# Experts of a two-layer model: the token blocks of an expert share each weight unit in turn, one code arm for each count class

## The chip, the cores and the metric

The kernel runs on one core of one Trainium2 chip. The metric is device microseconds of one execution, the median of several runs of the same program.

## The reference

Two layers of a hybrid model. Each mixes tokens (gated linear attention, differential attention, pooling) and then sends every token through two of sixteen experts. The first layer does so for 1280 tokens (256 context, 1024 latent), the second for the 1024 latent ones. Only the expert part matters here, cut to its core:

```python
def hier_moe(h, wg, bg, we, be, w1, w3, w2):        # h (N, 1024)
    g_prob = softmax(h @ wg + bg)                    # 4 groups, the best is taken
    e_prob = softmax(logits of the 4 experts in that group)   # the best 2 are taken
    weights = g_top * e_top / sum(e_top)
    ...                                              # assignments sorted by expert
    yb = (silu(x @ w1[e]) * (x @ w3[e])) @ w2[e]     # w1, w3 (1024, 512), w2 (512, 1024)
    out.at[token].add(yb * weight)                   # each token: sum over its experts
```

All of it is float32. How many rows an expert gets is known only at run time.

## The kernel before

A float32 product is made of three fast ones. `split` (L63, L64) writes a high part (ScalarE copy to the matmul's rounded type) and a low part (VectorE, value less high part); `mm3` (L67 to L69) adds high x high, high x low and low x high in PSUM.

For each layer the router leaves the list of rows of each expert and its count in memory. The stage then goes through the 16 experts in a fixed order. The weights of one expert are 12 units of 128 x 1024 numbers (512 KB): 0 to 3 and 4 to 7 hold w1 and w3 for the two halves of the hidden width, 8 to 11 hold w2. `fetch` has SyncE load a unit into one of 8 buffers `eraw`; `load_unit` has ScalarE copy its high part (L1579) and VectorE, for every third unit GpSimd, subtract the low part (L1581), into one of 13 buffers `ew`.

The rows of an expert are worked in blocks of 128. Block 0 (`x0`) always runs. The extra rows have their own blocks ahead of it: over 192 rows a full block 1; over 320 a full block 2, between 256 and 320 a 64-row block 2; between 128 and 192 a 64-row block 1. The prediction names the classes by their blocks: f (one full block), fh (a full and a 64-row one), ff, ffh, fff. Branches at run time (lines L1821, L1831, L1853, L1856 in the profile) choose, on each engine for itself. Rows beyond 384 go through a loop that this input never enters.

`gather` fetches a block's rows (GpSimd, indirect DMA) into `xg`. `prep` turns them: four TensorE transposes for each half (L1609) into a PSUM tile `xtp`, split by ScalarE and VectorE into `x`. A second VectorE instruction (L1611, CAST) copies 64 rows of the low part beside the high part, which only a 64-row block reads: it multiplies both parts in one pass (`pass2`). `prep` runs for blocks 0 and 1 of every expert, and for block 2 over 192 rows, whether the block is used or not.

`block` runs a full block through all 12 units. After units 0 to 3 ScalarE and VectorE make `g` = silu(h1) x h3 (L1653, L1654), TensorE turns `g` (L1636) in the middle of the next units, and the split is `ghl`. So there is a chain of TensorE, ScalarE, VectorE, TensorE, ScalarE, VectorE, TensorE for each half, the second of which ends at units 8 to 11. At the end VectorE weighs the result and GpSimd adds the rows to the output by an indirect DMA (L1626).

Only during block 0, the last of its expert, does `side(u)` load the 12 units of the next expert (one for each unit used), turn its blocks 0 and 1 at units 4, 5, 8 and 9, and issue gathers. `tc.manual_schedule()` keeps every engine's instructions in the order written:

```python
at = (6, 7, 9, 10) if ei == 0 else (4, 5, 8, 9)
if u in at:
    j, q = divmod(at.index(u), 2)
    if q == 0:
        nx["p"] = prep(gg[j], (x2, x1)[j])
    nx["p"](q, ("xtp", "hpse")[q])
```

Of the kernel before, what the change touches and what calls it, by code (L numbers as in the profile page):

```python
# [20 lines left out]
P = 128  # L21
# [34 lines left out]
def backbone_kernel(ctx: ExitStack, tc: tile.TileContext, x, ctx_in, cond, w_mod, b_mod, norm1, norm2, w_in_t, w_in_vg,  # L56
# [91 lines left out]
    for l in range(depth):  # L148
# [717 lines left out]
        ast, pst = ExitStack(), ExitStack()  # L866
        with ExitStack() as st:
# [685 lines left out]
        with ExitStack() as st:  # L1553
# [3 lines left out]
            RAW = 8  # L1557
            YT = 3
            early = True
            xg2 = mp1.tile([P, D], F32, name="xg2")  # L1560
# [4 lines left out]
            eo = [EPG * g + i for i in range(EPG) for g in (0, 2, 1, 3)]  # L1565
            seq = [(e, u) for e in eo for u in range(NUNIT)]
            raws = []

            def fetch():
                if seq:  # L1570
                    e, u = seq.pop(0)
                    raw = wk.tile([P, D], F32, name="eraw", tag="eraw", bufs=RAW)
                    nc.sync.dma_start(out=raw, in_=experts[l, e, u])
                    raws.append(raw)
# [12 lines left out]
            for _ in range(RAW):  # L1587
                fetch()
            def gather(idx, tag):
                g = wk.tile([P, D], F32, name="xg", tag=tag, bufs=YT if tag == "yt" else 1)  # L1590
                nc.gpsimd.indirect_dma_start(out=g, out_offset=None, in_=h2s,
                                             in_offset=bass.IndirectOffsetOnAxis(ap=idx, axis=0))
                return g

            gg = [None, None]
            for b in (1, 0):
                gg[b] = gather(ix[:, eo[0] + b * NE:eo[0] + b * NE + 1], f"xg{b}")
            units = [load_unit(u, False, nc.gpsimd if u in (3, 6) else nc.vector) for u in range(7)]
            for _ in range(7):
                fetch()  # L1600
            xt_ = [[mp1.tile([P, KD, n], F32R, name=f"x{n}{i}") for n in (P + P // 2, P)] for i in range(3)]

            def prep(g, xt):
# [17 lines left out]
            def scatter(yt, y, n, w, yidx):  # L1621
# [401 lines left out]
```

## Time and profile before

| | |
|---|---|
| median of 3 runs | 2952.78 us (2952.75 to 2956.32) |
| span of the profiled execution | 2951.4 us |
| TensorE busy | 2558.9 us, 87% |
| VectorE busy | 1911.1 us, 65% |
| ScalarE busy | 1243.7 us, 42% |
| GpSimd busy | 865.3 us, 29% |
| mean granted TensorE clock | 0.928 of full |
| expert stage, layer 0 | 936.5 to 1559.8 us of the span |
| expert stage, layer 1 | 2340.8 to 2920.5 us |

The profile is of one execution, so its span is compared with itself and the median stands beside it. The page's busy times are of all stages, and what bounds the experts is read in their two stretches: what each engine does there, what TensorE waits for, and what ends the wait. In rows with "<-" the name behind the arrow released the engine named ahead of it; "PEq" is TensorE's own sequencer, whose branches are listed as "PEldq COMPARE_BRANCH".

### The profile page before, as it was taken

Reading aid. Unit: us, or ns where it says so; the run is one execution under the profiler, and the core shown is the slowest. Engines: PE = TensorE matmul, PEld = TensorE weight load, DVE = VectorE, ACT = ScalarE, POOL = GpSimd, SP = SyncE. Lnnn points to the kernel's source line nnn. Section 1 sums busy time; section 2 is a strip of 40 time slices with the busy share of each in tenths; the row PEclk is TensorE's granted clock in tenths of the full one; section 3 lists DMA queues with packets and bytes.
Section 4 is the critical chain, followed back from the end, with each engine's and each line's share of the span. In section 5 each row is a group of like instructions: output and inputs, shape, how many; then the busy total and the mean of one; then the engine's idle time right before and its main releaser. Section 6 shows DMA issues by size and latency. Waiting matters only on the chain. (4 is left out here: it accounts for less than half of the span.)

```text
span 2951.4 us, 41503 instructions
## 1 busy us (share of the span) xinstructions
PE 2558.9 (87%) x15412; PEld 2145.6 (73%) x15412; DVE 1911.1 (65%) x3175; ACT 1243.7 (42%) x2060; POOL 865.3 (29%) x576
## 2 busy tenths in 40 slices
PE   6999998888896888789887999979989787978885
PEld 4878888887785667667666898868978566756664
DVE  3305765767578777876874317758867767687775
ACT  3322214665235444544554322137643354445453
POOL 0001113302244444443440001122024444454442
PEclk8999999999897999899998999989989888989997
DMA  8372227321336666776766252273122668587765
GB/s 286 131 259 104 76 77 191 69 65 51 116 128 230 217 212 201 243 239 183 233 191 214 84 178 76 80 178 77 42 94 104 229 192 288 174 301 235 236 216 196
DMA packets 159574, 494.08 MB, mean 167 GB/s; under 512 B 18896, under 2 KB 40016, under 8 KB 158768
## 3 DMA queue, kind: packets, MB, share of 16 engines
q1 hardware_dynamic: 110336, 361.14, 37.0%
q0 software_dynamic: 29312, 99.39, 12.1%
q10 hardware_dynamic: 19552, 28.84, 2.7%
q8 instruction: 201, 3.29, 0.5%
q14 instruction: 173, 1.42, 0.1%
HBM read 408.75 MB, written 79.15 MB: 165 GB/s over the span
## 5 line engine op out<-in xcount | busy, mean ns | idle before, releaser
L1581 DVE TENSOR_TENSOR ew<-eraw,ew 128x1024 fp32r<-128x1024 f32 x256 | 408.7, 1615 | 46.8 <-ACT ew L1579 39.9
L1579 ACT ACTIVATE ew<-eraw 128x1024 fp32r<-128x1024 f32 x384 | 390.4, 1053 | 107.1 <-PE hps L69 90.1
L1581 POOL TENSOR_TENSOR ew<-eraw,ew 128x1024 fp32r<-128x1024 f32 x128 | 331.4, 2598 | 126.9 <-issue 84.6
L67 PE MATMUL hps<-ew,x 128*128 128x512 f32 x656 | 280.0, 427 | 79.8 <-PEq L1856 75.7
L212 PE MATMUL ps<-hh,w 128*128 128x256 f32 x2096 | 287.2, 291 | 18.1 <-ACT hh L319 5.5
L212 PEld LDWEIGHTS ps<-hh,w 128*128 128x128 f32 x2096 | 267.4, 196 | 27.5 <-issue 7.9
L69 PE MATMUL hps<-ew,x 128*128 128x512 f32 x656 | 269.2, 410 | 10.7 <-DVE x L64 6.8
L68 PE MATMUL hps<-ew,x 128*128 128x512 f32 x656 | 269.1, 410 | 1.4 <-issue 1.4
L962 DVE TENSOR_REDUCE mx<-S 128x1 f32<-128x1280 f32 (+1 forms) x144 | 196.9, 1370 | 106.7 <-PE S L957 105.2
L1626 POOL DMA_INDIRECT xb<-yt,yx x54 | 131.7, 2440 | 412.5 <-DVE yt L1625 231.3
L67 PEld LDWEIGHTS hps<-ew,x 128*128 128x128 f32 x656 | 131.5, 200 | 114.4 <-issue 87.5
L970 ACT ACTIVATE pe<-S,mx 128x1280 f32<-128x1280 f32 (+1 forms) x144 | 177.5, 1232 | 48.2 <-DVE mx L962 40.9
L1611 DVE CAST x<-x 128x256 fp32r<-128x256 f32 x146 | 177.5, 1216 | 5.0
L956 PE MATMUL S<-kk,qh 128*128 128x512 f32 (+1 forms) x400 | 159.5, 399 | 16.0 <-DMA qh<-qs 7.8
L69 PE MATMUL yps<-ew,ghl 128*128 128x512 f32 x328 | 137.6, 420 | 40.6 <-DVE ghl L64 40.6
L69 PEld LDWEIGHTS hps<-ew,x 128*128 128x128 f32 x656 | 130.9, 200 | 45.2 <-DVE x L64 8.1
L68 PEld LDWEIGHTS hps<-ew,x 128*128 128x128 f32 x656 | 132.0, 201 | 26.7
L212 PE MATMUL ps<-hl,w 128*128 128x256 f32 x1048 | 149.7, 286 | 0.0
L67 PE MATMUL yps<-ew,ghl 128*128 128x512 f32 x328 | 143.3, 437 | 0.0
L67 PE MATMUL ps<-wv,hh 128*128 128x256 f32 (+1 forms) x480 | 142.2, 296 | 0.0
L957 PE MATMUL S<-kk,ql 128*128 128x512 f32 (+1 forms) x400 | 141.7, 368 | 0.3 <-DMA ql<-qs 0.3
L69 PE MATMUL ps<-wv,hl 128*128 128x256 f32 (+1 forms) x480 | 138.0, 288 | 0.0
(597 smaller groups left out, 5841.8 us busy)
## 6 DMA issues: line engine op xcount, KB each, us to landing
eraw<-in_experts_dram SPq DMA_DIRECT2D x384, 512.0 KB
s<-in_w_mod_dram SPq DMA_DIRECT2D x91, 512.0 KB
raw<-in_w_in_t_dram SPq DMA_DIRECT2D x28, 512.0 KB
xb<-xt POOLq DMA_DIRECT2D x18, 512.0 KB, 2.9
h2s<-tm POOLq DMA_DIRECT2D x18, 512.0 KB, 2.9
kk<-ks SPq DMA_DIRECT2D x14, 640.0 KB
ks<-shl ACTq DMA_DIRECT2D x16, 512.0 KB
qs<-shl ACTq DMA_DIRECT2D x16, 512.0 KB
```

The source lines that it names most:

```text
L67: nc.tensor.matmul(o, lhsT=lh, rhs=rh, start=start, stop=False)
L68: nc.tensor.matmul(o, lhsT=lh, rhs=rl, start=False, stop=False)
L69: nc.tensor.matmul(o, lhsT=ll, rhs=rh, start=False, stop=stop)
L212: nc.tensor.matmul(ps[:, o:o + 256], lhsT=wt[:, w_, k, :], rhs=h_[ci][:, k, :], start=w_ == 0 and h_ is hh and k == 0, stop=h_ is hl and k ...
L956: nc.tensor.matmul(S[:, j, :n], lhsT=qh[:, m, q1], rhs=kk[:, m, k0:k0 + n], start=True, stop=False)
L957: nc.tensor.matmul(S[:, j, :n], lhsT=ql[:, m, q1], rhs=kk[:, m, k0:k0 + n], start=False, stop=True)
L962: nc.vector.tensor_reduce(out=u["mx", m], in_=u["S", m], axis=AX.X, op=OP.max, negate=True)
L970: nc.scalar.activation(out=pe[:, :nk], in_=u["S", m], func=AF.Exp, bias=u["mx", m], scale=1.0, accum_out=acc)
L1579: nc.scalar.activation(out=w[:, 0, :], in_=raw, func=AF.Copy)
L1581: eng.tensor_tensor(out=w[:, 1, :], in0=raw, in1=w[:, 0, :].bitcast(F32), op=OP.subtract)
L1611: nc.vector.tensor_copy(out=xt[0][:, 4 * j:4 * j + 4, 0:P // 2], in_=xl[:, 4 * j:4 * j + 4, 0:P // 2].bitcast(F32))
L1626: nc.gpsimd.indirect_dma_start(out=xb, out_offset=bass.IndirectOffsetOnAxis(ap=yidx[0:n], axis=0), in_=yt[0:n], in_offset=None, compute_op ...
```

## The change

Each engine's code for an expert is now five arms, one for each class (fff, ffh, ff, fh, f), and one is run. In an arm, `run` goes through the units in steps: in step s block 0 does unit s, block 1 unit s - 1, block 2 unit s - 2. When the last block has used a unit, `after` loads the next expert's unit into the same buffer: the buffers are fixed tiles, 8 `eraw` and 12 `ew`. `Block` holds what `block` and `block_half` did; `pair` has the two forms of product. A 64-row block has tiles of its own layout, high rows 0 to 63 and low rows 64 to 127 of one tile (`x` and `ghl`), so the CAST is gone.

`turn_x` takes the place of `prep`. Block 0 of the next expert is turned at units 8 and 9. Blocks 1 and 2 are turned inside their own arm, in steps 0 and 1, and only where the arm has them; all turns use one PSUM tile `xtp`. The gather of the next expert's block 0 is issued at unit 9 of the expert before, two ahead. The last expert of layer 1, whose block 0 is worked into the final normalization, keeps its extra blocks ahead of block 0 (`extra`). An arm other than the last ends with a jump over the arms behind it, and each expert begins with the load of the next count into a register on each engine, which stood in block 0 before.

```diff
--- before.py
+++ after.py
...
+            RAW, NEW, YT, R = 8, 12, 3, P // 2
+            raw_t = [mp1.tile([P, D], F32, name=f"eraw{i}") for i in range(RAW)]
+            ew_t = [mp1.tile([P, 2, D], F32R, name=f"ew{i}") for i in range(NEW)]
+            xg_t = [mp1.tile([P, D], F32, name=f"xg{i}") for i in range(3)]
+            x0_t = [mp1.tile([P, KD, 2 * P], F32R, name=f"x0{i}") for i in range(2)]
+            xe_t = [None] + [mp1.tile([P, KD, 2 * P], F32R, name=f"xe{i}") for i in (1, 2)]
...
-            def load_unit(u, more=True, eng=None):
-                raw = raws.pop(0)
-                w = wk.tile([P, 2, D], F32R, name="ew", tag="ew", bufs=13)
...
+            acc = [pm_.tile([P, 2, 512], F32, name=f"acc{i}") for i in range(3)]
+
+            def fetch(i):
+                if i < len(flat):
+                    nc.sync.dma_start(out=raw_t[i % RAW], in_=experts[l, flat[i][0], flat[i][1]])
+
+            def load_unit(i, more=True, eng=None):
+                if i >= len(flat):
+                    return
+                raw, w = raw_t[i % RAW], ew_t[i % NEW]
                 nc.scalar.activation(out=w[:, 0, :], in_=raw, func=AF.Copy)
-                eng = eng or (nc.gpsimd if u % 3 == 2 else nc.vector)
+                eng = eng or (nc.gpsimd if i % 3 == 2 else nc.vector)
                 eng.tensor_tensor(out=w[:, 1, :], in0=raw, in1=w[:, 0, :].bitcast(F32), op=OP.subtract)
                 if more:
-                    fetch()
-                return w
+                    fetch(i + RAW)
...
-                xh, xl = xt[0][:, :, P // 2:], xt[1]
-
-                def half(j, tag="xtp"):
-                    tp = pm_.tile([P, 4, P], F32, name="xtp", tag=tag, bufs=1 if tag == "xtp" else 2)
-                    for i in range(4):
-                        nc.tensor.transpose(tp[:, i, :], g[:, (4 * j + i) * P:(4 * j + i + 1) * P], ident)
-                    split(xh[:, 4 * j:4 * j + 4, :], xl[:, 4 * j:4 * j + 4, :], tp)
-                    nc.vector.tensor_copy(out=xt[0][:, 4 * j:4 * j + 4, 0:P // 2], in_=xl[:, 4 * j:4 * j + 4, 0:P // 2].bitcast(F32))
-                return half
...
+            def turn_x(g, xt, j, n=P):
+                tp = pm_.tile([P, 4, P], F32, name="xtp", tag="xtp", bufs=1)[:, :, 0:n]
+                for i in range(4):
+                    nc.tensor.transpose(tp[:, i, :], g[0:n, (4 * j + i) * P:(4 * j + i + 1) * P], ident[0:n, 0:n])
+                split(xt[:, 4 * j:4 * j + 4, 0:n], xt[:, 4 * j:4 * j + 4, n:2 * n], tp)
...
+                def pair(self, o, hi, lo, both, wh, wl, start, stop):
+                    if self.full:
+                        mm3(o, hi, lo, wh, wl, start, stop)
+                        return
+                    if not stop:
+                        nc.tensor.matmul(o, lhsT=both, rhs=wh, start=start, stop=False)
+                    nc.tensor.matmul(o[0:R], lhsT=hi, rhs=wl, start=False, stop=False)
+                    if stop:
+                        nc.tensor.matmul(o, lhsT=both, rhs=wh, start=start, stop=True)
+
+                def mm(self, u):
+                    w = self.unit(u)
+                    n = P if self.full else R
+                    if u < 8:
+                        for i in range(2):
+                            k = 2 * (u % 4) + i
+                            cs_ = slice(i * 512, (i + 1) * 512)
+                            self.pair(self.h[u // 4], self.xt[:, k, 0:n], self.xt[:, k, n:2 * n], self.xt[:, k, 0:2 * n],
+                                      w[:, 0, cs_], w[:, 1, cs_], k == 0, k == KD - 1)
...
+            def run(blocks, before, after):
+                nb = len(blocks)
+                for s in range(NUNIT + nb - 1):
+                    for b in blocks:
+                        u = s - b.p
+                        if not 0 <= u < NUNIT:
+                            continue
+                        if b.p == 0:
+                            before(s, 0)
+                        b.mm(u)
+                        if b.p == 0:
+                            before(s, 1)
                         if u == 3:
...
+                            b.act(0)
+                        elif u == 5:
+                            b.turn_g(0)
+                        elif u == 7:
+                            b.act(1)
+                        elif u == 8:
+                            b.turn_g(1)
+                        elif u == 10:
+                            b.gain()
+                        elif u == 11:
+                            b.out()
+                        if b.p == 0:
+                            before(s, 2)
+                    after(s)
+                after(NUNIT + nb - 1)
...
+            def arm(ei, kinds):
+                if len(kinds) > 2 and kinds[2] == "f":
+                    overflow(ei)
+                blocks = blocks_of(ei, kinds)
+                nb = len(blocks)
+
+                def before(s, q):
+                    b = s + 1
+                    if b < 3 and q == 0 and b < nb:
+                        turn_x(xg_t[b], xe_t[b], 0, P if blocks[b].full else R)
+                    if b < 3 and q == 1:
+                        if b < nb:
+                            turn_x(xg_t[b], xe_t[b], 1, P if blocks[b].full else R)
+                        gather(ei + 1, b)
+                    if ei + 1 < NE and q == 2 and s in (8, 9):
+                        turn_x(xg_t[0], x0_t[(ei + 1) % 2], s - 8)
+                        if s == 9:
+                            gather(ei + 2, 0)
+
+                def after(s):
+                    if 0 <= s - nb < NUNIT:
+                        load_unit(ei * NUNIT + s - nb + NEW)
+                run(blocks, before, after)
...
-                x0, x1, x2 = xt_[ei % 2], xt_[2], xt_[(ei + 1) % 2]
-                with tc.If(cnt > P + P // 2) as big:
...
-                    block(x1, units, sw[:, col(e, 1)], swc[:, col(e, 1)], yx[:, col(e, 1)], side1, "e")
-                    with tc.If(cnt > 2 * P + P // 2) as big2:
-                        block(x2, units, sw[:, col(e, 2)], swc[:, col(e, 2)], yx[:, col(e, 2)], idle, "e")
...
-                with big.Else():
-                    with tc.If(cnt > P):
-                        block_half(x1, units, sw[:, col(e, 1)], swc[:, col(e, 1)], yx[:, col(e, 1)])
...
+                    nxc = nc.values_load(cnt_i[0:1, f:f + 1], min_val=0, max_val=cap)
+                fin_ = last and ei + 1 == NE
+                with tc.If(cnt > P + R) as c1:
+                    with tc.If(cnt > 2 * P) as c2:
+                        with tc.If(cnt > 2 * P + R) as c3:
+                            extra(ei, "ff") if fin_ else arm(ei, "fff")
+                        with c3.Else():
+                            extra(ei, "fh") if fin_ else arm(ei, "ffh")
+                    with c2.Else():
+                        extra(ei, "f") if fin_ else arm(ei, "ff")
+                with c1.Else():
+                    with tc.If(cnt > P) as c4:
+                        extra(ei, "h") if fin_ else arm(ei, "fh")
+                    if not fin_:
+                        with c4.Else():
+                            arm(ei, "f")
```

A single-block expert on VectorE, in the middle of layer 0, before. L64 is the subtract of a split (of x, or of the turned half `ghl`), L1581 of a weight unit:

```order
L64 TENSOR_TENSOR x_11586<-xtp,x_11585 128x512
L1611 CAST x_11585<-x_11586 128x4x64
L64 TENSOR_TENSOR ghl<-gtp,ghl 128x256
L64 TENSOR_TENSOR x_11586<-xtp,x_11585 128x512
L1611 CAST x_11585<-x_11586 128x4x64
L1654 TENSOR_TENSOR g<-g,hps 128x256
L1581 TENSOR_TENSOR ew<-eraw,ew 128x1024
L64 TENSOR_TENSOR ghl<-gtp,ghl 128x256
L1581 TENSOR_TENSOR ew<-eraw,ew 128x1024
L64 TENSOR_TENSOR x_11590<-xtp,x_11589 128x512
L1611 CAST x_11589<-x_11590 128x4x64
L64 TENSOR_TENSOR x_11590<-xtp,x_11589 128x512
```

and the arm of one full block after. L1677 makes `g`, L1617 and L1624 are the gain and the weighing of the result:

```order
L1581 TENSOR_TENSOR ew_11536<-eraw_11524,ew_11536 128x1024
L1677 TENSOR_TENSOR g<-g,acc_11555 128x256
L1581 TENSOR_TENSOR ew_11538<-eraw_11526,ew_11538 128x1024
L64 TENSOR_TENSOR ghl<-gtp,ghl 128x2x128
L64 TENSOR_TENSOR x_11548<-xtp,x_11548 128x4x128
L1581 TENSOR_TENSOR ew_11539<-eraw_11527,ew_11539 128x1024
L64 TENSOR_TENSOR x_11548<-xtp,x_11548 128x4x128
L1617 SCALAR_TENSOR_TENSOR yt<-g_11551,sw,yt 128x1024
L1581 TENSOR_TENSOR ew_11541<-eraw_11529,ew_11541 128x1024
L1624 TENSOR_TENSOR yt<-acc_11556,yt 128x1024
L1581 TENSOR_TENSOR ew_11542<-eraw_11530,ew_11542 128x1024
```

The casts are gone, and one block's turn stands here where two stood: of the four splits of `x` in the rows before (two blocks), two remain.

TensorE from the end of one expert into the next, before. `yps` is the second product's sum, `hps` the first's; L1821 is the branch on the count:

```order
L67 MATMUL yps<-ew,ghl 128x512
L68 MATMUL yps<-ew,ghl 128x512
L69 MATMUL yps<-ew,ghl 128x512
L1821 COMPARE_AND_BRANCH
L67 MATMUL hps<-ew,x_11589 128x512
L68 MATMUL hps<-ew,x_11589 128x512
L69 MATMUL hps<-ew,x_11590 128x512
```

and after, from the end of an fh arm. The numbered `acc` are PSUM tiles. L1892, L1893 and L1894 are the conditions on 192, 256 and 320 rows, L1901 that on 128, and L1832 that of the overflow loop:

```order
L67 MATMUL acc_11556<-ew_11543,ghl 128x512
L68 MATMUL acc_11556<-ew_11543,ghl 128x512
L69 MATMUL acc_11556<-ew_11543,ghl 128x512
L1901 UNCONDITIONAL_BRANCH
L1890 TENSOR_LOAD cnt_i
L1892 COMPARE_AND_BRANCH
L1893 COMPARE_AND_BRANCH
L1894 COMPARE_AND_BRANCH
L1832 COMPARE_AND_BRANCH
```

Between two experts' products now stand the jump out of the arm, the load and the nested conditions. Which of them are met depends on the class: an f expert takes the jumps at L1892 and at L1901.

TensorE's transposes, before, near the end of a block 0 for the next expert:

```order
L1609 MATMUL xtp<-cs,xg 128x128 x4
L67 MATMUL yps<-ew,ghl 128x512
L68 MATMUL yps<-ew,ghl 128x512
L69 MATMUL yps<-ew,ghl 128x512
L67 MATMUL yps<-ew,ghl 128x512
L68 MATMUL yps<-ew,ghl 128x512
L69 MATMUL yps<-ew,ghl 128x512
L1609 MATMUL xtp<-cs,xg 128x128 x4
```

and after, at the start of a three-block arm (ffh), for blocks 1 and 2 of the same expert:

```order
L1610 MATMUL xtp<-cs,xg_11545 128x128 x4
L67 MATMUL acc_11554<-ew_11532,x_11548 128x512
L68 MATMUL acc_11554<-ew_11532,x_11548 128x512
L69 MATMUL acc_11554<-ew_11532,x_11548 128x512
L67 MATMUL acc_11554<-ew_11532,x_11548 128x512
L68 MATMUL acc_11554<-ew_11532,x_11548 128x512
L69 MATMUL acc_11554<-ew_11532,x_11548 128x512
L1610 MATMUL xtp<-cs,xg_11545 128x128 x4
L1610 MATMUL xtp<-cs,xg_11546 128x64 x4
L67 MATMUL acc_11554<-ew_11533,x_11548 128x512
```

The second half of block 1 and the first half of block 2 now stand side by side, on one tile `xtp`.

## Rows read from the trace of the kernel before

**Rows 1.** Busy time by stretch (the two expert stages); the header names columns.

```profile
core 0: us, PE busy (x) PEld busy (x) DVE busy (x) ACT busy (x) POOL busy (x), PEclk, DMA share, GB/s
936.50:1559.80 623.30, 538.60 (x2436) 423.86 (x2436) 464.15 (x491) 308.70 (x450) 271.99 (x135) 0.92 0.70 221
2340.80:2920.50 579.70, 484.66 (x2186) 375.58 (x2184) 401.89 (x446) 277.64 (x414) 266.04 (x135) 0.91 0.71 231
```

**Rows 2.** Waits of TensorE, layer 0: total us, times, the longest us.

```profile
PE hps L67 <- PEq L1856: 35.2, 8, 7.4
PE yps L69 <- DVE ghl L64: 29.2, 11, 3.7
PE gtp L1636 <- DVE g L1654: 9.1, 3, 4.4
PE hps L69 <- DVE x L64: 6.8, 2, 5.2
```

**Rows 3.** Waits of TensorE, layer 1.

```profile
PE hps L67 <- PEq L1856: 40.5, 7, 8.5
PE gtp L1636 <- DVE g L1654: 11.9, 10, 3.5
PE yps L69 <- DVE ghl L64: 11.4, 6, 3.0
...
PE xtp L1609 <- DMA xg<-h2s,ix: 5.4, 1, 5.4
PE hps L1686 <- issue: 4.3, 1, 4.3
```

**Rows 4.** Timeline about 1036 us: start, duration, engine, line, operation, tiles.

```profile
1036.10 4.98 DVE L1611 CAST x<-x 128x256 fp32r<-128x256 f32 x1
...
1036.27 4.65 POOL L1581 TENSOR_TENSOR ew<-eraw,ew 128x1024 fp32r<-128x1024 f32 x2
...
1041.34 1.21 DVE L1581 TENSOR_TENSOR ew<-eraw,ew 128x1024 fp32r<-128x1024 f32 x1
```

**Rows 5.** Instruction groups by line, layer 0: busy us, mean ns, idle before.

```profile
L1611 DVE CAST x<-x 128x256 fp32r<-128x256 f32 x72 | 99.5, 1382 | 2.5
```

**Rows 6.** Branch lines on TensorE's sequencer: ns least/median/most, first and last start.

```profile
L1853 PEldq COMPARE_BRANCH  x18: 65/183/3127, 980.7 to 2810.3; - x18
...
L1853 PEldq EVENT_SEMAPHORE  x2: 51/51/51, 1306.0 to 2369.0; - x2
...
L1856 PEldq COMPARE_BRANCH  x30: 82/236/6041, 932.9 to 2901.0; - x30
...
L1856 PEldq EVENT_SEMAPHORE  x16: 51/51/51, 936.4 to 2901.4; - x16
...
L1821 PEldq COMPARE_BRANCH  x32: 70/4590/7651, 928.5 to 2897.5; - x32
```

**Rows 7.** TensorE's timeline from one single-block expert into the next.

```profile
1180.13 0.60 PE L1609 MATMUL xtp<-cs,xg 128*128 128x128 f32 x4
1180.49 0.48 PE L67 MATMUL yps<-ew,ghl 128*128 128x512 f32 x1
...
1182.90 0.39 PE L68 MATMUL yps<-ew,ghl 128*128 128x512 f32 x1
1183.13 0.40 PE L69 MATMUL yps<-ew,ghl 128*128 128x512 f32 x1
1190.95 0.77 PE L67 MATMUL hps<-ew,x 128*128 128x512 f32 x1 [7.42 <-PEq L1856]
```

**Rows 8.** Instructions of the tile xtp, layer 0: ns least/median/most.

```profile
L63 ACT ACTIVATE x<-xtp x72: 578/590/602, 949.8 to 1535.9; 128x512 fp32r<-128x512 f32 x72
L64 DVE TENSOR_TENSOR x<-xtp,x x72: 673/681/693, 950.4 to 1538.6; 128x512 fp32r<-128x512 f32 x72
```

**Rows 9.** The two branches at that boundary, by line.

```profile
L1821 PEldq COMPARE_BRANCH  x1: 6388/6388/6388, 1179.7 to 1179.7; - x1
...
L1856 PEldq COMPARE_BRANCH  x1: 4641/4641/4641, 1186.1 to 1186.1; - x1
```

**Rows 10.** Load of a count on TensorE's sequencer, by line.

```profile
L1871 PEldq TENSOR_LOAD <-cnt_i x30: 298/307/1139, 936.6 to 2879.2; - x30
```

More of the change, by code (lines that the diff above doesn't have):

```diff
@@ L1564, in backbone_kernel @@
             swc = sw if last else mp1.tile([P, NB * NE], F32, name="swc")
[L1565 to L1574, printed above, removed]
@@ new lines, in backbone_kernel @@
+            for b in range(3):
+                gather(0, b)
+            for i in range(7):
+                load_unit(i, False, nc.gpsimd if i in (3, 6) else nc.vector)
+            for i in range(7):
+                fetch(RAW + i)
+            def turn_x(g, xt, j, n=P):
[3 more added lines that the diff above has]
+                split(xt[:, 4 * j:4 * j + 4, 0:n], xt[:, 4 * j:4 * j + 4, n:2 * n], tp)
@@ new lines, in nothing, with blocks_of @@
+            def nothing(*a):
+                pass
+            def blocks_of(ei, kinds, b0=0):
+                e, nb = eo[ei], len(kinds)
+                return [Block(p, nb, k == "f", x0_t[ei % 2] if p + b0 == 0 else xe_t[p + b0], ei * NUNIT,
+                              sw[:, col(e, p + b0)], None if last else swc[:, col(e, p + b0)], yx[:, col(e, p + b0)])
+                        for p, k in enumerate(kinds)]
+            for j in range(2):
+                turn_x(xg_t[0], x0_t[0], j)
+            gather(1, 0)
@@ L1738, in backbone_kernel @@
+            for i in range(7, NEW):
+                load_unit(i)
             for c in g2b:
@@ new lines, in overflow @@
+            def overflow(ei):
+                e = eo[ei]
+                with tc.If(cnt > 3 * P):
+                    for t in tiles:
+                        for j in range(2):
+                            nc.gpsimd.indirect_dma_start(
+                                out=slots, out_offset=bass.IndirectOffsetOnAxis(ap=di[:, t, j:j + 1], axis=0),
+                                in_=sva[:, t, j, 1:4], in_offset=None)
+                    with tc.For_i(e * cap + 3 * P, e * cap + cnt, P) as i:
+                        sd = wk.tile([P, 3], F32, name="sd", tag="sd", bufs=1)
+                        nc.sync.dma_start(out=sd, in_=slots[bass.ds(i, P), :])
+                        si = wk.tile([P, 2], I32, name="si", tag="si", bufs=1)
+                        nc.vector.tensor_copy(out=si, in_=sd[:, 0:2])
+                        g = wk.tile([P, D], F32, name="xo", tag="yt", bufs=YT)
+                        gather_to(g, si[:, 0:1])
+                        for j in range(2):
+                            turn_x(g, xe_t[1], j)
+                        if not last:
+                            nc.vector.tensor_scalar(out=sd[:, 0:1], in0=sd[:, 0:1], scalar1=float(NCTX), scalar2=None, op0=OP.is_lt)
+                            nc.vector.tensor_tensor(out=sd[:, 1:2], in0=sd[:, 0:1], in1=sd[:, 2:3], op=OP.mult)
+                            nc.vector.tensor_tensor(out=sd[:, 2:3], in0=sd[:, 2:3], in1=sd[:, 1:2], op=OP.subtract)
+                        run([Block(0, 1, True, xe_t[1], ei * NUNIT, sd[:, 2:3], sd[:, 1:2], si[:, 1:2])], nothing, nothing)
@@ new lines, in extra @@
+            def extra(ei, kinds):
+                if kinds[-1] == "f" and len(kinds) == 2:
+                    overflow(ei)
+                blocks = blocks_of(ei, kinds, 1)
+                for b in blocks:
+                    for j in range(2):
+                        turn_x(xg_t[b.p + 1], xe_t[b.p + 1], j, P if b.full else R)
+                run(blocks, nothing, nothing)
+            cnt = nc.values_load(cnt_i[0:1, eo[0]:eo[0] + 1], min_val=0, max_val=cap)
+            for ei, e in enumerate(eo):
+                if ei + 1 < NE:
+                    f = eo[ei + 1]
+                    nxc = nc.values_load(cnt_i[0:1, f:f + 1], min_val=0, max_val=cap)
[14 more added lines that the diff above has]
+                            arm(ei, "f")
+                if fin_:
+                    blk = blocks_of(ei, "f")
+                    blk[0].out = lambda: fix(blk[0])
+                    run(blk, nothing, ending)
@@ L1884, in backbone_kernel @@
                 if ei + 1 < NE:
-                    units, cnt = nxt, nx["c"]
+                    cnt = nxc
             if last:
```

263 lines of the change are left out of this document (78 added, 185 removed).

## The prediction

> **What bounds the kernel now.** I read the busy time by stretch first. The two expert stages take 623.3 and 579.7 us, 1203.0 us of the profiled execution's span of 2951.4, and the change touches only them. TensorE's matmuls run for 538.6 and 484.7 us of that, more than any other engine [rows 1]. So the stages are bound by TensorE, and what can be won or lost is its idle time and its instructions. The waits of TensorE come next [rows 2, 3]. They fall into two kinds. At the start of a main block it waits for its own sequencer: 35.2 and 40.5 us, 15 waits. Inside blocks it waits for the chain that turns a hidden half round (VectorE's product g, transposes, the split into ghl): 29.2 + 9.1 us in layer 0 and 11.9 + 11.4 in layer 1, together 61.6 us in 30 waits.
>
> The timeline shows why that chain is late: a cast L1611 lasts 4.98 us beside a GpSimd subtract of 4.65, and the product g can only start after it. The same VectorE does a weight subtract in 1.21 us when it is alone [rows 4]. All casts of the layer-0 stage hold VectorE for 99.5 us [rows 5].
>
> The branch rows give the expert classes [rows 6]. 16 jumps past the 64-row block are single-block experts (f). L1853 runs twice in each expert over 192 rows: 18 runs, so 9 experts, of which 2 jump past the 64-row block (ff) and 7 don't (ffh). 32 counts in all leave 7 experts of one full and one 64-row block (fh). By the times of these rows 5 of the f follow an ffh or ff, 9 follow an f or fh, one begins layer 0 and one ends layer 1.
>
> **The change part by part.** The sum is made against the span, 2951.4 us; the median of the runs shown is 1.4 above it and is kept above it.
>
> *Transposes.* Before, every expert's blocks 0 and 1 are turned (and block 2 over 192), whether needed or not: 2 x 32 + 9 = 73 blocks. After, each arm turns its own: 32 + 7 + 2 + 14 = 55. A half block's four transposes move TensorE on by 0.36 us (1180.13 to 1180.49) [rows 7]. 18 x 2 x 0.36 = **-13**.
>
> *Chain waits.* The casts go; a 64-row block now reads high and low part from one tile of its own layout. A single-block arm gives VectorE 8 subtracts, 2 splits of x and no cast where it had 8, 4 and 4. The GpSimd subtracts stay, and so does their hold on VectorE's subtracts (4.65 against 1.21 [rows 4] is the pair's worst), so I take two thirds of 61.6 as gone: **-45**; the ends are 0 and -62. In the arms of two or three blocks the other blocks' matmuls stand between g and its use, which helps.
>
> *Clock after a wait.* The first matmul behind the 7.42 us wait lasts 0.77 us, the last ahead of it 0.40 [rows 7]. A slow one costs 0.37; I put 0.5 us, a little over one of them, on each wait that goes, 20 of the 30: **-10**, between 0 and -15.
>
> *Other waits for x.* 6.8 us for the split of x and 5.4 for a gathered row block [rows 2, 3]: the next expert's turn keeps its place (units 8 and 9) with half the VectorE work around it, and gathers start a block earlier: **-12**, between 0 and -12.
>
> *New waits at the start of an arm.* One PSUM tile takes every turn now, where two alternated. In a three-block arm the second half of block 1 and the first of block 2 are turned back to back, so the second group waits for ScalarE's and VectorE's splits, 0.59 + 0.68 us [rows 8], with hops about 2. Queued behind it on TensorE is the whole arm. In the 9 arms over 192 rows and the 7 fh also stands a shorter one, about 1 us where only 6 matmuls lie between the halves. 7 x 2 + 9 x 1 = **+23**, taking the 7 fh as hidden. The ends are 0 (the splits come first in both queues) and 50, where a VectorE subtract of 1.2 to 3 us stands ahead of each of 25 splits.
>
> *Branches.* This is the dear part. A far jump costs between 3.1 (the dearest of the 18 of L1853, just its fetch) and 7.65 us (the dearest of L1821); a near one 0.08 to 0.24 [rows 6]. The sequencer meets it some 3.8 us ahead of the matrix work: L1821 starts at 1179.7, the last matmul before it ends at 1183.5 [rows 7, 9]. So the price is what exceeds 3.8: 6.39 + 4.64 make the 7.42 seen. After, the program holds five arms for each expert, and its order on TensorE is: far jump out of an arm (over the arms behind it), a load of the count, then c1, c2, c3, c4 as nested.
> - 5 f behind ffh or ff: the jump out 3.3 (near the 3.1 of L1853, also a jump past a block), the load 0.3 [rows 10], c1 4.5 and c4 4.0 (below the single 4.64, since a fetch has just ended), less 3.7: 8.4 each, 42.
> - 9 f behind f or fh: c1 5.5 (between the median 4.59 and the 6.39), c4 4.2, load 0.3, less 3.7: 6.3 each, 57.
> - With some 5 for the last expert, whose branches stay: 104 against 75.7 before, **+28**.
> - 9 arms of ff and ffh: one far jump into the arm, 4.5 + 0.3 and 0.8 for the near ones, less 3.8, is 1.8 each, 16. Four "issue" waits of the kind of the 4.3 [rows 3] stand at these experts before; I let 4 us of them go: **+12**.
> - 7 fh: before only c1; now 4 of them come behind a far jump out, 2 each, the other 3 pay the load: **+9**.
> Together +50 rounded. If every jump were near, the 75.7 would go and it would be about -75; with 5.5 for each far jump it is +96 (5 f at 13.0, 9 at 7.5 and the last one against 75.7: +62; 9 arms at 2.2 less 4: +16; 4 fh at 4.2 and a load more for the others: +18).
> The same jumps on VectorE, ScalarE and GpSimd lie beside TensorE's; were they as dear, they would end no later than TensorE's own. What hides under them is the weight supply: a buffer filled during the last arm is already there.
>
> [...]
>
> [...]
>
> *Fixed buffers and the sends.* Twelve weight buffers for thirteen; the next expert's unit is copied when the last block has used the buffer. A single-block arm is 72 matmuls, 0.23 us apart (1182.90 to 1183.13 [rows 7]), and 12 transposes, some 18 us in all, and a buffer's new content is wanted one arm later, so the copy (about 1 us) and subtract are hidden. Cost 0; if the cover goes, rival 3. In a three-block arm three sends stand on GpSimd's queue, with its next subtracts behind them; these are due an arm later.
>
> Sum: -13 - 45 - 10 - 12 + 23 + 50 - 4 = -11: a span of 2940.4, and with the 1.4 **2942 us**.
>
> **The rivals.**
> 1. *Slower: the jumps decide.* TensorE's sequencer pays 5.5 us at every far jump, also where one follows another within a few instructions. For: L1821 and L1856 stand behind one another as c1 and c4 will, and their dearest are 7.65 and 6.04 [rows 6]. Against: the medians are 4.59 and 0.24. Price: branches +96 for +50 and some 5 of slow clock behind the longer waits: 2942 + 51 = **2993 us**. It decides from 5 us a jump on.
> 2. *Much faster: VectorE was the only trouble.* All 62 us of chain waits go (17 more), with the clock behind them (5), the new waits halve (11), and the jumps out of the arms turn out near (5 x 3 + 4). For: VectorE's casts are 99.5 us in a layer [rows 5]. Against: the GpSimd subtracts remain. 2942 - 52 = **2890 us**.
> 3. *No gain: supply.* Single-block arms stay bound by the weights: the stage in layer 1 moves 231 GB/s at a DMA share of 0.71 [rows 1], so full share gives 325 GB/s, and an expert's 12 x 0.524 MB need 19.4 us. That is near the 18 of TensorE's work, and the splits share three engines on top. The f arms would keep their time: the jump loss of the f (+28), most of the saved transposes and two thirds of the chain and clock gain vanish under the supply. What stays is +12 + 9 in branches, the new waits by half (+11), -15 and -3 of chain and clock, -12 and -4: -2, or **2951 us**. Against: no wait of TensorE on a weight DMA is among its waits in either layer [rows 2, 3].
>
> **How the numbers follow.** Forecast 0.37 (its own range 2918 to 2965: chain and new waits at their ends by half), rival 1 0.28, rival 2 0.26, rival 3 0.09. About 0.2%, 6 us, is what a measurement can tell. Of the forecast 0.24 is faster, 0.08 same, 0.05 slower. Rival 1 is slower, rival 2 faster, rival 3 mostly same (0.05) with 0.02 to each side. Faster 0.52, same 0.13, slower 0.35. The range of 2874 to 2995 leaves out the half of rival 1 that is dearer still, and the cheap end of rival 2, some 2 in 10 together.
>
> **What would show it.** Right: no cast on VectorE, TensorE's waits on g and ghl at about 20 us instead of 62, its waits on its sequencer at about 130 us, 55 blocks' transposes, and waits on the turned x at the start of three-block arms near 2 us. Wrong: a jump's median away from 4.5 us, waits for ew at all (supply), chain waits above 40 us.

## The result, and the profile after

The changed kernel takes 3102.45 us (median of 4 runs, 3090.79 to 3104.64) against 2952.77 us: the ratio is 1.0505, 95% interval 1.0477 to 1.0534. It is slower by 5%, outside the range of the prediction. The profiled execution has a span of 3102.8 us, 151 more than before.

First the busy time in the two expert stages, from the first weight matmul to the last as in [rows 1]; the columns are the same.

```profile
942.00:1638.30 696.30, 537.97 (x2260) 407.49 (x2260) 360.86 (x387) 294.37 (x410) 251.54 (x133) 0.89 0.63 189
2438.30:3072.40 634.10, 482.17 (x2006) 364.38 (x2004) 307.20 (x343) 260.17 (x370) 247.26 (x132) 0.87 0.69 212
```

The stages grew from 1203.0 to 1330.4 us. TensorE is busy for 1020.1 us where it was 1023.3, although it runs fewer instructions: its granted clock fell from 0.92 and 0.91 to 0.89 and 0.87. VectorE is busy for 668 us, not 866. So the engine that was to be relieved was relieved, and TensorE idles 130 us more. What it waits for, in layer 0 and then in layer 1, as in [rows 2, 3]:

```profile
PE acc L67 <- issue: 78.9, 7, 14.8
PE xtp L1610 <- DVE xe L64: 20.3, 12, 3.3
PE xtp L1610 <- DVE x L64: 10.6, 5, 4.2
PE acc L1650 <- DVE g L1677: 9.6, 9, 1.3
PE acc L67 <- DVE hs L1682: 7.3, 5, 1.5
PE acc L67 <- DVE g L1677: 7.2, 7, 1.6
PE xtp L1610 <- DVE yt L1617: 7.0, 3, 2.9
...
PE gtp L1692 <- DVE g L1677: 5.7, 3, 2.2
```

```profile
PE acc L67 <- issue: 62.3, 7, 11.3
PE xtp L1610 <- DVE ew L1581: 14.5, 2, 7.3
PE acc L1650 <- DVE g L1677: 13.2, 12, 1.3
PE xtp L1610 <- DMA xb<-yt,yx: 11.4, 2, 5.8
PE xtp L1610 <- DVE xe L64: 9.1, 2, 5.9
```

The first row of each is the start of single-block arms, but for one wait of 1.1 us ("issue": nothing but the sequencer). Other rows hold waits for branches too: the longest for "DVE ew L1581" ends 0.3 us after a branch of TensorE's sequencer. One start of a single-block arm, on TensorE's timeline, and its branches by line:

```profile
1121.96 0.40 PE L1653 MATMUL acc<-ew,ghl 128*128 128x512 f32 x1
1135.43 0.77 PE L67 MATMUL acc<-ew,x 128*128 128x512 f32 x1 [13.07 <-issue]
1135.99 0.63 PE L68 MATMUL acc<-ew,x 128*128 128x512 f32 x1
```

```profile
L1894 PEldq COMPARE_BRANCH  x1: 4764/4764/4764, 1118.1 to 1118.1; - x1
...
L1890 PEldq TENSOR_LOAD <-cnt_i x1: 1172/1172/1172, 1122.9 to 1122.9; - x1
...
L1892 PEldq COMPARE_BRANCH  x1: 5680/5680/5680, 1124.2 to 1124.2; - x1
...
L1901 PEldq COMPARE_BRANCH  x1: 5327/5327/5327, 1129.9 to 1129.9; - x1
```

The jump out of the ffh arm (4.76), the load (1.17, not 0.3) and two jumps (5.68, 5.33) make 16.9 us, and stand between 1118.1 and 1135.3. TensorE's last matmul ended 4.3 us after the first of them began; the rest, 13.07, is idle, and the matmuls behind it run slow (0.77 and 0.63 against 0.40; the granted clock from 1135.4 to 1139.0 was 0.50). [Rows 7] shows a later boundary, also from an ffh expert into a single-block one, not from one single-block expert into the next. The two boundaries, the one of 13.07 and that of [rows 7], cost 2.70 and 7.42 before,

```profile
1104.48 0.77 PE L67 MATMUL hps<-ew,x 128*128 128x512 f32 x1 [2.70 <-PEq L1856]
```

and 13.07 and 14.84 after:

```profile
1232.83 0.76 PE L67 MATMUL acc<-ew,x 128*128 128x512 f32 x1 [14.84 <-issue]
```

I added up every idle stretch of TensorE over 0.1 us in the expert stages of each trace, together with the waits just ahead of a stage's first weight matmul (6.5 us before, 19.0 after). One counts as a branch wait if its next matmul starts within 0.7 us after a branch of TensorE's sequencer ends, whatever releaser the waits view infers.

| TensorE waits, us, both layers | before | after |
|---|---|---|
| branches | 97.5 | 192.9 |
| turns and x | 12.7 | 75.1 |
| chain of g and ghl | 65.8 | 10.6 |
| a block's matmul, on g or hs of another block | 0 | 44.6 |
| other | 9.5 | 6.0 |
| sum | 185.5 | 329.2 |

The difference is 144 of the 151 us, 12.5 of it ahead of the stages, with 3 less of busy time. Of the other 10 us, 8.6 stand right behind layer 0: the next stage's first matmul waits 9.9 us for a DMA, where it waited 1.3.

### The profile page after: what moved, and what is told of

Its sections match the earlier page's. It is cut to its first block, busy times and chain, and to the rows that moved or that the text cites. A ratio compares the mean times of both kernels' runs of the same rounds, so it can differ in the third digit from the quotient of the medians.

```text
span 3102.8 us, 40369 instructions
## 1 busy us (share of the span) xinstructions
PE 2564.5 (83%) x15044; PEld 2117.7 (68%) x15044; DVE 1715.3 (55%) x2965; ACT 1216.9 (39%) x1979; POOL 837.5 (27%) x576
## 5 line engine op out<-in xcount | busy, mean ns | idle before, releaser
L1581 DVE TENSOR_TENSOR ew<-eraw,ew 128x1024 fp32r<-128x1024 f32 x256 | 390.5, 1530 | 224.5 <-ACT ew L1579 211.8
L1579 ACT ACTIVATE ew<-eraw 128x1024 fp32r<-128x1024 f32 x384 | 392.5, 1050 | 162.9 <-PE acc L69 132.4
L1581 POOL TENSOR_TENSOR ew<-eraw,ew 128x1024 fp32r<-128x1024 f32 x128 | 339.3, 2653 | 379.7 <-ACT ew L1579 378.0
L67 PE MATMUL acc<-ew,x 128*128 128x512 f32 x512 | 236.0, 461 | 165.1 <-issue 141.2
L67 PEld LDWEIGHTS acc<-ew,x 128*128 128x128 f32 x512 | 111.2, 217 | 202.9 <-issue 162.1
L68 PE MATMUL acc<-ew,x 128*128 128x512 f32 x512 | 224.2, 438 | 0.0
L69 PE MATMUL acc<-ew,x 128*128 128x512 f32 x512 | 223.1, 436 | 0.0
L1610 PE MATMUL xtp<-cs,xg 128*128 128x128 f32 (+1 forms) x440 | 75.7, 305 | 133.3 <-DVE xe L64 29.4
L1627 POOL DMA_INDIRECT xb<-yt,yx x54 | 105.5, 1954 | 268.5 <-DVE yt L1624 88.7
L1610 PEld LDWEIGHTS xtp<-cs,xg 128*128 128x128 f32 (+1 forms) x440 | 55.5, 166 | 164.6 <-issue 97.4
L1593 POOL DMA_INDIRECT xg<-h2s,ix x96 | 106.9, 1113 | 185.5 <-PE xtp L1610 111.2
L67 PE MATMUL ps<-wv,hh 128*128 128x256 f32 (+1 forms) x480 | 142.1, 296 | 0.0
L212 PEld LDWEIGHTS ps<-hl,w 128*128 128x128 f32 x1048 | 138.5, 196 | 0.0
L69 PE MATMUL ps<-wv,hl 128*128 128x256 f32 (+1 forms) x480 | 138.0, 288 | 0.0
L68 PE MATMUL ps<-wv,hh 128*128 128x256 f32 (+1 forms) x480 | 137.8, 287 | 0.0
```

The source lines that it names most:

```text
L67: nc.tensor.matmul(o, lhsT=lh, rhs=rh, start=start, stop=False)
L68: nc.tensor.matmul(o, lhsT=lh, rhs=rl, start=False, stop=False)
L69: nc.tensor.matmul(o, lhsT=ll, rhs=rh, start=False, stop=stop)
L212: nc.tensor.matmul(ps[:, o:o + 256], lhsT=wt[:, w_, k, :], rhs=h_[ci][:, k, :], start=w_ == 0 and h_ is hh and k == 0, stop=h_ is hl and k ...
L1610: nc.tensor.transpose(tp[:, i, :], g[0:n, (4 * j + i) * P:(4 * j + i + 1) * P], ident[0:n, 0:n])
```

## The experiments

"Fixed path" means that the choice by count is left out: the program holds only the arms that this input takes, by a table of its classes (`CLASSES`). Ratios are to the kernel before, with 95% intervals. Waits of a kind are counted as in the table above. "..." marks code left out of an edit.

**The jumps.** Fixed path of the changed kernel, and of the kernel before:

```diff
-                with tc.If(cnt > P + R) as c1:
...
+                if not fin_:
+                    arm(ei, CLASSES[l][ei])
...
```

> The changed kernel with the run-time choice left out: each expert's arm is written straight into the program for this input's counts, so no jump and no join is left. Theory (far jumps plus waits on the one turn tile): the 193 us of branch waits go, and some 20 us of waits at the joins with them: about 2890 us. Rival (the weave of blocks through each unit is itself the slower order, the jumps only lie beside it): not under 3010 us.

> The kernel before with the run-time choice left out in the same way. Theory: its 98 us of branch waits go, 2855 us. The difference to the changed kernel on a fixed path is then what the change does without jumps: theory +35 us (turn waits of about 63 more, chain waits of 12 less, 15 of transposes), rival +150 us as now.

Measured: 2953.06 us (1.001, 0.9993 to 1.0028) and 2880.03 (0.9747, 0.971 to 0.9784). The choice costs the changed kernel 149 us and the kernel before 69. Without it the changed kernel is still 73 us slower. The first time lies midway between theory and rival, the second 25 us above the theory: half of the loss is jumps, half is not. On the fixed path waits for VectorE came up where jumps had hidden them, in layer 0:

```profile
PE xtp L1611 <- DVE xe L65: 43.3, 13, 6.3
PE gtp L1693 <- DVE g L1678: 26.2, 10, 5.2
```

The first was 20.3 us with jumps, the second 5.7.

**One jump for a single-block expert.** In the changed kernel, and the same in the kernel before:

```diff
+                with tc.If(cnt > P) as c0:
+                    with tc.If(cnt > P + R) as c1:
...
+                if not fin_:
+                    with c0.Else():
+                        arm(ei, "f")
```

> The changed kernel with the test on 128 rows outermost: a single-block expert takes one far jump into its arm and not two. Theory: 14 experts lose a jump of some 5.5 us that nothing hides: -75, about 3027 us. Rival (the second jump lies in the shadow of the first fetch or of other waits): -20 at the most, 3080 us or more.

> The kernel before with the test on 128 rows outermost: a single-block expert takes one far jump where it took two. Its second jump (L1856) cost 4.4 us in 10 of 16 cases. Theory (what a jump less gives is partly taken back by VectorE's lag, as in the changed kernel): about -25, 2925 us. Rival (full gain): -45, 2905 us.

Measured: 3067.97 us (1.0382, 1.034 to 1.0424) and 2944.36 (0.9995, 0.9976 to 1.0015). The jumps went as expected: by the count above branch waits fell from 192.9 to 102.4 and from 97.5 to 50.0. The time did not follow: the changed kernel came out nearer the rival, and the kernel before did not move, which neither expectation had. Of its 47 us at the branches, 29 came back as waits for g and ghl and 5 as waits for the turned x (the profiled executions differ by 10 us, the medians hardly). In layer 1 now:

```profile
PE gtp L1636 <- DVE g L1654: 31.4, 12, 4.8
PE hps L67 <- PEq L1821: 14.1, 6, 4.0
```

against 11.9 and 40.5 in [rows 3]. So VectorE caught up while TensorE waited at its branches, and without that it was late. In the changed kernel the waits for g and ghl rose by 28 us, from 10.6 to 39.0.

**The turn tile and the PSUM tiles.** Alternating a second turn tile (half of an `acc` that is free at that time; the second half of the next block 0's turn gets one too, in arms of one or two blocks), and a PSUM tile for each block:

```diff
...
-                            turn_x(xg_t[b], xe_t[b], 1, P if blocks[b].full else R)
+                            turn_x(xg_t[b], xe_t[b], 1, P if blocks[b].full else R, acc[b][:, 1, :])
...
```

```diff
-                    if nb <= 2:
+                    if nb == 1:
                         self.h = [acc[0][:, p, :], acc[1][:, p, :]]
-                        self.y = acc[2 if p == 0 else 1]
+                        self.y = acc[2]
                     else:
-                        self.h = [acc[p // 2][:, p % 2, :], acc[(p + 3) // 2][:, (p + 3) % 2, :]]
+                        self.h = [acc[p][:, 0, :], acc[p][:, 1, :]]
                         self.y = acc[p]
```

> The changed kernel with the second half of a turn put in a PSUM bank that is free at that time, so that two turn tiles alternate. Theory (the turns wait for the split of the one tile): TensorE's waits at the transposes fall from 75 to about 30 us, -45, 3057 us. Rival (these waits are waits at the joins, for the last VectorE work and the last send of the arm before): -10 or less, 3090 us.

> The changed kernel in which each block of a two- or three-block arm has a PSUM tile of its own for its sums, where before two blocks had halves of one tile. Theory (a block's matmul waits while ScalarE and VectorE read the other half of its tile): the waits of TensorE's block matmuls on g and hs, 45 us in 39 cases, go: about 3060 us. Rival (the same time is waited for at the next step of the chain): 3090 us or more.

> The changed kernel on a fixed path (no jump) and with two turn tiles. Its waits at the transposes were 97 us on the fixed path with one tile. Theory (one turn tile, its split late on VectorE, is what the weave lost beside the jumps): about 60 of them go, 2893 us, near the 2880 of the kernel before on a fixed path. Rival (the weave itself, its chain of g and VectorE's lag at the start of an arm): 2935 us or more.

Measured: 3065.96 us (1.0387, 1.0354 to 1.0419), 3050.77 (1.0348, 1.0294 to 1.0402), and on the fixed path 2917.38 (0.9902, 0.9865 to 0.9939): 36, 52 and, from 2953, 36 us. The first two came out near their theories, the third midway between theory and rival. The own tiles were worth the most of the three mends and were no term of the prediction. The changed kernel's timeline at 1273 us shows why:

```profile
1272.10 0.39 PE L69 MATMUL acc<-ew,x 128*128 128x512 f32 x1
1272.53 0.38 ACT L1676 ACTIVATE g<-acc 128x256 f32<-128x256 f32 x1 [3.47 <-PE acc L69]
...
1272.94 0.42 DVE L1677 TENSOR_TENSOR g<-g,acc 128x256 f32<-128x256 f32 x1 [2.63 <-ACT g L1676]
1273.42 0.50 PE L1650 MATMUL acc<-ew,xe 128*128 128x512 f32 x1 [0.93 <-DVE g L1677]
```

Block 0's first sum is done and is read by L1676 and L1677. Block 1's matmul writes the other half of the same tile, and starts only after the read. With own tiles this row is gone, and of all waits of block matmuls on g or hs 3 us remain.

The turn tile is seen at the start of an ffh arm of the changed kernel, at 1065 us:

```profile
1065.01 1.21 DVE L1624 TENSOR_TENSOR yt<-acc,yt 128x1024 f32<-128x1024 f32 x1
1065.04 0.60 ACT L63 ACTIVATE xe<-xtp 128x512 fp32r<-128x512 f32 x1 [0.75 <-PE xtp L1610]
...
1066.14 1.21 DVE L1581 TENSOR_TENSOR ew<-eraw,ew 128x1024 fp32r<-128x1024 f32 x1
...
1067.28 0.68 DVE L64 TENSOR_TENSOR xe<-xtp,xe 128x512 fp32r<-128x512 f32 x1
1068.01 0.66 PE L1610 MATMUL xtp<-cs,xg 128*128 128x128 f32 x4 [0.53 <-DVE xe L64]
...
1069.39 0.69 DVE L64 TENSOR_TENSOR xe<-xtp,xe 128x512 fp32r<-128x512 f32 x1 [1.44 <-ACT xe L63]
1070.14 0.46 PE L1610 MATMUL xtp<-cs,xg 64*128 64x64 f32 x4 [1.47 <-DVE xe L64]
```

ScalarE has its half of the split done at 1065.64, but on VectorE the weighing and a subtract of the arm before stand ahead of it; the next turn starts only at 1068.01, and the one behind that waits 1.47 us for its split.

**The mends together.** First one jump with two turn tiles; then one jump and own PSUM tiles with the turn halves of blocks 1 and 2 spread over steps 0 to 3 (a second turn tile only in single-block arms); then own tiles and spread turns on the fixed path:

> The changed kernel with both edits: the test on 128 rows outermost and two turn tiles. Theory (the two waits stand at different places): the gains of 35 and 36 us add up, 3031 us. Rival (each edit uncovers VectorE's lag that the other's wait had covered): 3050 us. Opposite case (with the split no longer waited for, the jump's part counts in full): 2995 us.

> The changed kernel with one jump for the single-block experts, own PSUM tiles, and the halves of the turns of blocks 1 and 2 spread over steps 0 to 3 (a second turn tile in single-block arms). Theory: the waits are at different places, so about 3102 - 35 - 36 - 40 = 2990 us, still slower than the kernel before. Rival (VectorE's lag takes back what is freed): 3025 us.

> The changed kernel on a fixed path with own PSUM tiles and the spread turns. Theory (jumps, the one turn tile and the shared PSUM tiles are all that the weave lost): 2917 less some 40, about 2875 us, level with the kernel before on a fixed path (2880). Rival (the weave keeps a cost of its own, VectorE's lag at the change of arms): 2905 us or more.

Measured: 3036.13 us (1.0291, 1.0249 to 1.0334), 2994.67 (1.0141, 1.0086 to 1.0195), and on the fixed path 2884.39 (0.9781, 0.9739 to 0.9822). The gains nearly add up: 35 and 36 alone are 66 together, and with the 52 of the own tiles they are 108. On the fixed path the mended weave (the blocks' steps through each unit) is level with the kernel before (2880): theory, not rival. But the kernel before still has its casts there; without those of blocks 0 it takes 2843 (below), so the weave keeps a cost of some 40 us against the old order. Its waits for the turned x are still 85 us there. The 110 us between 2995 and 2884 are what the choice by count costs it still.

**The casts.** The kernel before without the casts of blocks 0, which no one reads, alone, with one jump, and on the fixed path:

```diff
...
-                    nc.vector.tensor_copy(out=xt[0][:, 4 * j:4 * j + 4, 0:P // 2], ...)
+                    if both:
+                        nc.vector.tensor_copy(out=xt[0][:, 4 * j:4 * j + 4, 0:P // 2], ...)
...
```

> The kernel before, in which the 128-row blocks 0, which never read the copied low part, leave out the VectorE cast (64 of its 146). Theory (casts make the chain of g late): TensorE's chain waits fall from 66 to about 40 us, about 2920 us. Rival (GpSimd's subtracts hold VectorE's subtracts as well, so the chain stays late): 2945 us.

> The kernel before without the casts of blocks 0 and with one jump for a single-block expert. Alone the casts gave 37 us and the jump nothing, because 47 us less at the branches came back as 47 us of waits for VectorE. Theory (VectorE's lag took it back, and without the casts it has less lag): the jump now counts, 2870 us. Rival (GpSimd's subtracts hold VectorE as much as the casts did): 2905 us, as without the jump edit.

> The kernel before on a fixed path and without the casts of blocks 0. On the fixed path it waited 128 us, nearly all for g and ghl. Theory (VectorE's lag from the casts): about 65 of them go, 2815 us, so that the weave on a fixed path with two turn tiles (2917) is 100 us slower than the old order of blocks with the same VectorE work. Rival: 2850 us.

Measured: 2909.23 us (0.9867, 0.9833 to 0.9901), 2907.23 (0.9865, 0.9812 to 0.9918), and 2842.82 (0.9635, 0.9586 to 0.9684). The first was as the theory had it, or better, the other two as the rival. In the first the waits for g and ghl fell from 66 to 17 us, but the branch waits rose from 98 to 130: much of what TensorE no longer waited for the chain it waited at its branches. In the second the chain waits were back at 40: something else still held VectorE, and the jump still gave nothing.

**GpSimd's subtracts.** All low parts of the weights on VectorE, in four kernels:

```diff
-                eng = eng or (nc.gpsimd if u % 3 == 2 else nc.vector)
+                eng = eng or nc.vector
```

> The kernel before without the casts of blocks 0, with one jump, and with all low parts of the weights subtracted on VectorE (GpSimd does none in the loop). Theory (VectorE is late because GpSimd's subtract holds it, 2.4 to 5 us at a time): the chain waits fall and the jump saved now counts, 2890 us. Rival (VectorE's own work in a single-block expert, 12 x 1.21 us and some 8 more, is what is late): 2930 us or more.

> The kernel before with that one edit alone, casts and two jumps left in. Theory (GpSimd's hold is the cause of the chain waits, the casts only a part of what was held): TensorE's 66 us of chain waits nearly all go, 2865 us. Rival (the casts' own time is still too much beside twelve subtracts): 2920 us or more.

> The changed kernel as it is, with all low parts of the weights subtracted on VectorE in the loop. In the kernel before (with two other edits) this gave 105 us. Theory (GpSimd's hold on VectorE makes the turns' splits late at the change of arms): the waits at the transposes fall by half or more, 3040 us. Rival (in the weave VectorE has work to spare, and jumps and PSUM tiles bind): 3085 us or more.

> The changed kernel with the three mends (one jump, own PSUM tiles, spread turns) and no GpSimd subtract. Theory: the 27 us of waits for VectorE that came back with the jump saved go, and the rest of the lag, 2925 us. Rival: 2970 us or more. Either stays behind 2803, if the jumps out of the arms (104 us of branch waits) are what the weave can't shed.

Measured: 2802.55 us (0.949, 0.9445 to 0.9535), 2858.38 (0.9688, 0.9667 to 0.9709), 3067.91 (1.0398, 1.0374 to 1.0422) and 2940.78 (0.9964, 0.9948 to 0.9981). In the kernel before this one line is worth 89 us, more than the whole choice by count; on top of the two other edits it gave 105, and 2803 is 87 us better than the theory had it; the second time is the theory's. Here are VectorE's subtracts and casts in the kernel before with that one edit:

```profile
L1581 DVE TENSOR_TENSOR ew<-eraw,ew 128x1024 fp32r<-128x1024 f32 x380 | 462.0, 1240 | 85.7 <-ACT ew L1579 78.3 <-DVEq L1856 4.5 <-issue 1.1
...
L1611 DVE CAST x<-x 128x256 fp32r<-128x256 f32 x146 | 45.4, 311 | 5.1
```

Before, VectorE's 256 subtracts took 1615 ns each and the casts 1216 ns:

```profile
L1581 DVE TENSOR_TENSOR ew<-eraw,ew 128x1024 fp32r<-128x1024 f32 x256 | 408.7, 1615 | 46.8 <-ACT ew L1579 39.9 <-DVEq L1856 4.9 <-DVEq L1853 0.8
...
L1611 DVE CAST x<-x 128x256 fp32r<-128x256 f32 x146 | 177.5, 1216 | 5.0
```

So 124 subtracts more cost VectorE 53 us, and the casts alone gave back 132. The chain waits of TensorE, 65.8 us, fell to 5.2, in layer 0 and layer 1:

```profile
PE gtp L1636 <- DVE g L1654: 4.0, 7, 0.6
```

```profile
PE gtp L1636 <- DVE g L1654: 1.2, 7, 0.2
```

The cast was never dear: it was held. In the changed kernel, where VectorE had less to do, the edit gave 35 us: its jumps were left, 203 us by the same count, and 44 us of waits at the PSUM tiles that two blocks share. The theory's 3040, with half of the waits at the turns gone, was too good there (about a third went); so was its 2925 for the mended weave.

The fastest kernel is thus the old order of blocks with three small edits, 2802.55 us, 5.1% faster than before. Its branch waits are 68 us; those of the mended weave without GpSimd's subtracts are 112, and its waits at the turns are still over 50.

## Why the prediction was wrong

Three steps failed, each by about as much: the price of the jumps (by 45 us), the new waits for turned rows (51), and PSUM tiles shared by two blocks (45), which were no term. They make 141 of the 160 us between 2942 and 3102.

- **Branches**: the term of +50 was +95. The price of a jump was taken as 3.3 to 4.5 us where jumps follow one another ("since a fetch has just ended"); they took 4.8, 5.7 and 5.3 at the place shown, with a load of 1.17 between them. So the five single-block experts behind an ffh waited 13.5 us each for 8.4 in the sum, and the nine behind an f or fh 7.9 for 6.3. The kernel before did have the cheaper second jump: 11 far jumps (over 1 us) that began within 1.5 us after another had a median of 3.8 us, the 28 others 5.4. In the changed kernel 25 such jumps had 5.4, the 32 others 4.9. Why the second jump is no cheaper there stays open. That a fetch just ended makes the next jump cheaper was my estimate. What the traces show is instruction traffic beside each jump: the page lists a DMA queue "q8 instruction" (226 packets, 3.70 MB in the changed kernel), and at least one packet of it moved during every one of the 57 far jumps, as in all 39 before; at the place shown it was one, two and one. Which engine's code it was they don't tell. Rival 1 had the mechanism and the size (+96), and its time was still 110 us short, since it kept the other terms.
- **New waits at the start of an arm**, +23 with -12 for the other waits for x, came to +62. The mechanism (one tile, splits late on VectorE) held: two tiles gave 36 us. I had counted a split's own time; what stood ahead of it was the end of the arm before, its weighing and subtracts, and in layer 1 twice a send (11.4 us). The term's dear end, 50 with a subtract ahead of each split, was the nearer one.
- **PSUM tiles that two blocks share**, +45, were missed. The kernel's text shows them: in an arm of two blocks both sum into halves of `acc[0]` and `acc[1]`.
- **Chain waits** fell by 55, against 45. The count was near, and leaving out casts does lower these waits (66 to 17 us in the kernel before). But a cast is dear only while GpSimd subtracts (before, all 59 casts that took over 0.6 us, 1.4 to 5.2, overlapped one; without GpSimd's subtracts a cast takes 0.31). The 4.98 us row of [rows 4] stands beside two GpSimd subtracts, 4.65 us together; I wrote of a hold on the subtracts and took the cast itself as a cause. How much of the 55 is the casts and how much the other blocks' matmuls between g and its use was not tried apart.
- **Transposes** (18 blocks fewer, as counted) and **64-row blocks** are small, and their effect on the time wasn't tried alone. No run shows the sum's last term, -4, for fewer and wider matmuls in the 64-row blocks: in the kernel before, their matmuls of 256 columns followed one another at 0.117 us and those of 512 at 0.23, so two of the narrow ones took as long as one of the wide. TensorE's busy time hardly fell, and the **clock** term, -10, went the other way: of the 2952 matmuls L67 to L69 on expert weights 344 lasted over 0.55 us, at a mean granted clock of 0.51, where 229 did before. At 0.43 us from one matmul to the next (1135.99 to 1136.42 us) for 0.23 in [rows 7], 115 more of them are some 23 us, an estimate.
- What the sum could not hold: the terms hide one another, though the three mends hardly do. A jump saved gave nothing in the kernel before, and 35 of 90 us in the changed one, as VectorE was late behind it.
- **Supply** (rival 3) played no part: the only wait of a weight matmul that the views of the changed kernel put down to a weight, 6.1 us on "ACT ew L1579", ends 0.2 us after a far jump, and the fixed path moved 238 GB/s in layer 1 against 212 with jumps.

## What to carry to other kernels

Before work is added to or taken from a loaded engine, ask what stretches its instructions: one that lasts four times its free time beside another engine's (the casts here, 1216 ns for 311) may be held by it, and then the cure is at the other engine, as it was here. Count the far jumps one after another that the commonest case takes, at the price measured for each (here a median of 5.4 us for one behind another, 3.8 in the kernel before) beyond the time that the sequencer runs ahead (here about 4 us), and test the commonest case first. Where two streams of work are woven, give each its own tile, also in PSUM (52 us here), and try each removed wait for what stood behind it before you count it as a gain.

## What the runs showed of the hardware

- GpSimd's 128 x 1024 subtract of two SBUF tiles holds VectorE so much that giving the work back to VectorE made it faster in all: casts 1216 to 311 ns, subtracts 1615 to 1240 ns, the kernel 3.1%. Few were held a little: before, 219 of the 256 subtracts took 1.1 to 1.3 us, 34 over 2.8 and three between. All 37 of the longer ones overlapped a GpSimd subtract, and 17 of the 219. By what means GpSimd holds VectorE no run shows.
- A count's register load on TensorE's sequencer took 1.14 to 1.18 us behind each of the five far jumps out of an ffh arm in layer 0, 0.30 and 0.71 behind the two in layer 1, and 0.30 to 0.32 elsewhere in the changed kernel.
- A far jump on TensorE paid its whole price right behind another in the changed kernel (median 5.4 us, against 4.9 alone), though not in the kernel before (3.8 against 5.4). A jump can also be near: the one out of an fh arm, over the f arm alone, took 0.31 to 0.33 us in all seven cases, the one over an fh arm into the f arm 3.5 to 8.5 in all 15. The rows of the changed kernel, least, median and most in ns, with the branches that are not taken (0.07 to 0.08 us) among them:

```profile
L1892 PEldq COMPARE_BRANCH  x32: 70/5032/6063, 931.6 to 3044.8; - x32
```

```profile
L1894 PEldq COMPARE_BRANCH  x14: 3809/4826/5673, 962.0 to 2965.4; - x14
```

```profile
L1901 PEldq COMPARE_BRANCH  x30: 70/3390/8482, 936.2 to 3048.7; - x30
```
